# RWKV-7 and windowed-attention block: low-rank decay and rate products over rounded parts, cumulative decay by a VectorE scan

## The chip, the cores and the metric

The kernel runs on one core of a Trainium2 chip. The time is the device time of one execution in microseconds (us), as the median of several executions. A profiled execution is one further execution of which every instruction was recorded. Its engines are PE (matrix products; PEld is its loading of weights), DVE or VectorE, ACT or ScalarE, POOL or GpSimd, and SP, which issues most loads.

## The reference

One decoder block over 512 tokens with 2048 channels: a projection of the normalised input, RWKV-7 time mixing and sliding-window attention in parallel, a gated merge, and a gated convolutional feed-forward layer. The part that matters is the start of the time mixing:

```python
r, k, v, wd, ad, gd = jnp.split(zs, [o1, o2, o3, o4, o5], axis=-1)
w = -jax.nn.softplus(-(w0 + jnp.tanh(wd) @ w2)) - 0.5
decay = jnp.exp(-jnp.exp(w.astype(f32)))
a = jax.nn.sigmoid(a0 + ad @ a2)
g = jax.nn.sigmoid(gd) @ g2
...
state = (state * w_t[:, :, None, :] + sa[..., None] * kb_t[:, :, None, :]
         + v_t[..., None] * k_t[:, :, None, :])
y = jnp.einsum('bhvk,bhk->bhv', state, r_t)
```

`tanh(wd) @ w2` is the low-rank product of the decay (rank 96 to 1024 channels), `ad @ a2` that of the rate (rank 96 to 1024). The kernel works the recurrence in chunks of 64 tokens, for which it needs, in each chunk, the running sum over tokens of the logarithm of the decay, and that sum's exponentials.

## The kernel before

Large products are made from rounded parts. A full-precision matrix is split into a rounded part "hi" (ACT, a copy to the type F32R) and the rest "lo" (DVE, a subtraction), and a product is the sum of three passes: hi with hi, hi with lo, lo with hi. For the projection, SP loads a piece of weights into `raw`, ACT makes `whi` (L254), DVE `wlo` (L255), and PE runs the three passes (L269 to L271) into `acc`. In the text these passes are "the stream". Four buffers each of `raw`, `whi` and `wlo` let loads and splits run ahead.

The kernel first norms and transposes the input, then does attention, then the time mixing, which is the stage of the change, and then the merge, the output product, the up-projection and the down-projection. The time mixing treats the 16 heads in eight pairs, 128 channels each. For a pair there are three steps.

- `early(p)` prepares. It loads `wl`, the pair's slices of the low-rank weights (L556; columns for the decay, the rate and two for the gate), splits the gate's two, projects k, r and v, and forms the decay, the rate and the scaled keys. The decay's product with `thw` (L576) is four full-precision matmuls that put tokens on the partitions; tanh (L578, ACT) and an addition (L579, DVE) follow; four more full-precision matmuls with the constant `tri` (L583) do the running sum inside each chunk and put channels on the partitions; two exponentials (L584 into `Et`, L586 into `Ei`) read it. The rate's product is one full-precision matmul of 512 columns (L589).
- `late(p)` builds the chunk matrices (`BAR`, `BKK`, L625 to L628, multiplied at L645), inverts a triangular matrix by doubling (L697 to L749), and then runs the chain over eight chunks. In each, PE makes `psG` (L757), DVE copies it to `GY` (L758), PE makes `psU` (L760), ACT and DVE copy it to `UV` (L761, L762), PE makes `psS` (L766), and DVE updates the state `SV` (L770). Each step waits for the one before.
- `final(p)` transposes the result (L798), multiplies by the gate (L812) and stores.

`early(p + 1)` is written between `late(p)` and `final(p)`, and a scheduler at build time interleaves the stream, the next pair's preparation and the chain in one fixed order for each engine. Engines run their own instructions in that order, each waiting for what it needs. Six entries of a pair (transposes and first products) are tied by hand to places in the stream (the lists FIRST, LATER and LAST).

`wl` has one buffer. POOL issues loads that add to what is in memory or in SBUF; they prepare sums of weights for later stages (L239) and inside the up-projection (L1102).

Of the kernel before, what the change touches and what calls it, by code (L numbers as in the profile page):

```python
# [18 lines left out]
P = 128  # L19
S = 512  # L20
NT = S // P
HD = 64
C = 64
# [5 lines left out]
SQE = float(np.exp(-0.5))  # L29
# [5 lines left out]
class Dims:  # L35
# [37 lines left out]
CONST_PARTS = (  # L73
    ("ident", 128), ("strict", 64), ("incl", 64), ("istack", 64),
    ("m1", 64), ("m2", 32), ("m4", 32), ("m8", 32), ("m16", 32), ("m32", 32),
    ("t1bd", 128), ("idsg", 128), ("tri", 128), ("bo", 128), ("sel2", 2), ("ones", 128), ("dist", 256),
)
CONST_AT = {}
_at = 0
# [6 lines left out]
def shape_constants():  # L86
    out = np.zeros((P, NCONST), np.float32)

    def put(nm, a):
        o, n = CONST_AT[nm]  # L90
        out[:, o : o + n] = a

    i = np.arange(P)
    put("ident", np.eye(P))
    s = (i % C)[:, None]
    t = np.arange(C)[None, :]
    put("strict", s < t)
    put("incl", s <= t)
    put("istack", SG * (s == t))
    put("idsg", SG * np.eye(P))  # L100
    for m in LEVELS:
        off = (s // (2 * m) == t // (2 * m)) & (s % (2 * m) < m) & (t % (2 * m) >= m)

        put(f"m{m}", SG * off if m == 1 else ((off | (s == t)) / SG)[:, t[0] % (2 * m) >= m])
    si, ti = i[:, None], i[None, :]
    put("t1bd", (si == ti) | ((si // 2 == ti // 2) & (si > ti)))
    same = si // C == ti // C
    put("tri", same & (si <= ti))
    put("bo", same)
    put("sel2", si // C == np.arange(2)[None, :])  # L110
    put("ones", 1.0)
    kj = np.arange(2 * BLK)[None, :]
    dist = (BLK + si - kj).astype(np.float32)
    put("dist", np.where((dist >= 0) & (dist < WIN), -dist, -1e32))
    return out
# [19 lines left out]
def block_kernel(ctx: ExitStack, tc: tile.TileContext, d: Dims, a: dict, out: bass.AP):  # L135
    nc = tc.nc
    act, dve, pool, pe, sync = nc.scalar, nc.vector, nc.gpsimd, nc.tensor, nc.sync
# [40 lines left out]
    K = {nm: cst[:, o - P : o - P + n] for nm, (o, n) in CONST_AT.items() if o}  # L178
# [32 lines left out]
    def split(hi, lo, src, pin=free):  # L211
        pin(act.activation(hi, src, AF.Copy))
        pin(dve.tensor_tensor(lo, src, hi.bitcast(F32) if hi.dtype == F32R else hi, op=ALU.subtract))
# [6 lines left out]
    for f in range(NPRE):  # L220
        w, t = a["w_up"][f], {n: up_d[f, n] for n in ("s3", "s1", "P6", "P3")}
# [70 lines left out]
    if True:  # L292
# [3 lines left out]
        with tc.tile_pool(name="x0_ps", bufs=6, space=PSUM) as ps0:  # L296
            ssum = p0.tile([P, NT], F32, name="ssum")
            HT = NT // 2
            for h in range(2):
# [3 lines left out]
                r = rsqrt_small(p0, ssum[:, h * HT : (h + 1) * HT], 1.0 / d.D, RMS_EPS)  # L303
# [3 lines left out]
            for h in range(2):  # L307
                hs = slice(h * HT * P, (h + 1) * HT * P)
                for k in range(NK):
                    ps = ps0.tile([P, HT * P], F32, name="ps_x", tag="x")  # L310
# [47 lines left out]
        with ExitStack() as pt:  # L358
# [32 lines left out]
            for t in range(NKV):  # L391
# [30 lines left out]
            for g in range(NHK):  # L422
# [7 lines left out]
                for n in range(NT):  # L430
                    ts = slice(n * P, (n + 1) * P)
# [54 lines left out]
        with ExitStack() as pr:  # L486
# [13 lines left out]
            def shifted(acc, mucol, dst, i):  # L500
                z = zpads[i]
                act.activation(z[:, 1:], acc, AF.Identity, scale=pcol[:, mucol : mucol + 1])
                dve.scalar_tensor_tensor(dst, acc, omu[:, mucol : mucol + 1], z[:, 0:S], op0=ALU.mult, op1=ALU.add)

            def wtile(tag, bufs=1):
                return wk.tile([P, S], F32, name=tag, tag=tag, bufs=bufs)

            def bulk():
                return blk.tile([P, S], F32, name="bulk", tag="bulk")

            NG = d.GL // P
            thw = lp.tile([P, S], F32, name="thw")
            adz = lp.tile([P, S], F32, name="adz")
            gdz = [lp.tile([P, NG, S], F32R, name=f"gd{e}") for e in ("hi", "lo")]
            bor = lp.tile([P, P], F32R, name="bor")
            dve.tensor_copy(bor, K["bo"])
            acc = ztile(d.c_wd)
            shifted(acc, PR["muwd"], thw, 0)
            act.activation(thw, thw, AF.Tanh)
            if d.DL < P:  # L520
                dve.memset(thw[d.DL : P], 0.0)
            dve.memset(thw[d.DL : d.DL + 1], 1.0)
            acc = ztile(d.c_ad)
            shifted(acc, PR["muad"], adz, 1)
            if d.AL < P:
                dve.memset(adz[d.AL : P], 0.0)
            for i in range(NG):
                acc = ztile(d.c_gd + i * P)
                t = wtile("lw")
                shifted(acc, PR["mugd"] + i, t, i % 2)  # L530
                act.activation(t, t, AF.Tanh, scale=0.5)
                dve.tensor_scalar(t, t, 0.5, 0.5, op0=ALU.mult, op1=ALU.add)
                split(gdz[0][:, i], gdz[1][:, i], t)
# [17 lines left out]
            def r3(ap, c=C):  # L551
                return ap.rearrange("p (n c) -> p n c", c=c)

            def early(p):
                wl = lp.tile([P, 2 + NG, P], F32, name="wl", tag="wl", bufs=1)
                sync.dma_start(wl, a["lora"][p].rearrange("p (k c) -> p k c", c=P))  # L556
                w2 = wl[:, 0]
                ag = [lp.tile([P, NG, P], F32R, name=f"w{e}", tag=f"w{e}", bufs=2) for e in ("ghi", "glo")]
                split(*ag, wl[:, 2:])

                sums_along(up_jobs)()
                acc = ztile(d.c_k + p * P)
                kz = wtile("kz")
                shifted(acc, PR["mu"] + NP + p, kz, 0)
                kk = wtile("kk")
                dve.tensor_scalar(kk, kz, col("k_k", p), None, op0=ALU.mult)
                sq = wtile("lg")
                act.activation(sq, kk, AF.Square)
                ps = bulk()
                head_stats(ps, sq)  # L570
                rs = rsqrt_small(wk, ps[:, 0 : 2 * NT], None, None, mx=1e-24)
                rb = head_rows(wk, bulk(), rs, "lg")
                ps = bulk()
                for t in range(NT):
                    ts = slice(t * P, (t + 1) * P)
                    pe.matmul(ps[:, ts], thw[:, ts], w2, start=True, stop=True)  # L576
                lg = wtile("lw")
                act.activation(lg, ps, AF.Tanh, scale=0.5)  # L578
                dve.tensor_scalar(lg, lg, 1.0, None, op0=ALU.add)  # L579
                ps = bulk()  # L580
                for t in range(NT):
                    ts = slice(t * P, (t + 1) * P)
                    pe.matmul(ps[:, ts], lg[:, ts], K["tri"], start=True, stop=True)  # L583
                act.activation(Et[:, :, 1:], r3(ps), AF.Exp, scale=-0.5 * SQE)  # L584
                Ei = wtile("Ei")
                act.activation(Ei, ps, AF.Exp, scale=0.5 * SQE)  # L586

                ps = bulk()
                pe.matmul(ps, wl[:, 1], adz, start=True, stop=True)  # L589
                ta = wtile("at_")  # L590
                act.activation(ta, ps, AF.Tanh, scale=0.5, bias=half[:, 0, p : p + 1])

                acc = ztile(d.c_r + p * P)
                rz = wtile("rz")
                shifted(acc, PR["mu"] + p, rz, 1)
                acc = ztile(d.c_v + p * P)
                vz = wtile("vz", 2)
                shifted(acc, PR["mu"] + 2 * NP + p, vz, 0)

                k2 = wtile("k2")  # L600
                dve.tensor_scalar(k2, ta, half[:, 1, p : p + 1], half[:, 2, p : p + 1], op0=ALU.mult, op1=ALU.add)
                dve.tensor_tensor(k2, k2, kz, op=ALU.mult)
                dve.tensor_scalar(ta, ta, 0.5, 0.5, op0=ALU.mult, op1=ALU.add)
                kb = kz
                rk = wtile("lw")
                dve.scalar_tensor_tensor(rk, rz, col("r_k", p), k2, op0=ALU.mult, op1=ALU.mult)
                rkl = [wk.tile([P, S], F32R, name=f"rk{e}", tag="rhl" if e else "dd") for e in range(2)]
                split(*rkl, rk)
                pin(dve.tensor_tensor(kk, kk, rb, op=ALU.mult))
                dve.tensor_tensor(kb, kk, ta, op=ALU.mult)  # L610
                ps = bulk()
                for e in range(2):
                    pe.matmul(ps, bor, rkl[e], start=e == 0, stop=e == 1)
                bon = wtile("bon", 2)
                dve.tensor_tensor(bon, vz, ps, op=ALU.mult)
                return ag, Ei, kk, kb, k2, rz, vz, bon
# [876 lines left out]
```

## Time and profile before

| | us |
|---|---|
| median of 3 runs | 2801.39 |
| lowest and highest | 2800.23, 2801.68 |
| the profiled execution | 2801.0 |
| its span, first to last instruction | 2799.2 |

In the profile, a row of a timeline has the start in us from the span's start, the time that it took, the engine, the line of the kernel, the operation, the tile written and the tiles read, the shape, and how many such instructions follow each other; in brackets stand the idle time of that engine just before, and what ended it. A row of a group has, after the bar, the total busy time in us and the mean of one in ns. Line numbers are those of the kernel before; in the excerpts of the new order they are up to a few lines off for the same statement (L269 to L271 there are L267 to L269, psG, psU and psS are L760, L763 and L769).

### The profile page before, as it was taken

Reading aid. Unit: us, or ns where it says so; the run is one execution under the profiler, and the core shown is the slowest. Engines: PE = TensorE matmul, PEld = TensorE weight load, DVE = VectorE, ACT = ScalarE, POOL = GpSimd, SP = SyncE. Lnnn points to the kernel's source line nnn. Section 1 sums busy time; section 2 is a strip of 40 time slices with the busy share of each in tenths; the row PEclk is TensorE's granted clock in tenths of the full one; section 3 lists DMA queues with packets and bytes.
Section 4 is the critical chain, followed back from the end, with each engine's and each line's share of the span. In section 5 each row is a group of like instructions: output and inputs, shape, how many; then the busy total and the mean of one; then the engine's idle time right before and its main releaser. Section 6 shows DMA issues by size and latency. Waiting matters only on the chain.

```text
span 2799.2 us, 45969 instructions
## 1 busy us (share of the span) xinstructions
PE 2755.7 (98%) x17466; PEld 2401.1 (86%) x17466; DVE 1985.3 (71%) x3452; ACT 1352.1 (48%) x2278; POOL 231.3 (8%) x307
## 2 busy tenths in 40 slices
PE   6999999999999999999999999999999999999999
PEld 5777788888878788888889999999999999888887
DVE  5588677877787774545678778787777778655555
ACT  4355445545544553322466554545555555444444
POOL 0001110110101001011000011101110101000000
PEclk9999999999999999999999999999999999999999
DMA  7865887777777777888776888888888888877775
GB/s 220 229 159 155 210 208 190 194 193 189 197 182 199 186 177 219 239 255 284 248 254 187 234 230 221 241 233 227 229 242 229 225 232 236 317 243 241 256 256 188
DMA packets 227182, 619.62 MB, mean 221 GB/s; under 512 B 24832, under 2 KB 44944, under 8 KB 225936
## 3 DMA queue, kind: packets, MB, share of 16 engines
q1 hardware_dynamic: 158400, 441.03, 48.2%
q0 software_dynamic: 37216, 136.33, 25.5%
q10 hardware_dynamic: 31344, 39.31, 4.0%
q8 instruction: 137, 2.24, 0.3%
q14 instruction: 85, 0.70, 0.1%
HBM read 566.96 MB, written 191.18 MB: 271 GB/s over the span
## 4 chain that ended last, share of the span: by engine, by line
PE 88%; DVE 6%; ACT 2%; issue 1%; DMA 1%; ACTq 0%; SPq 0%; DVEq 0%
PE X L1133 17%; PE X L997 11%; PE acc L271 10%; PE acc L270 10%; PE acc L269 10%; PE Y L997 9%; PE Y L1133 8%; PE Z L1133 4%; PE psS L766 1%; PE psG L757 1%; PE bulk L697 1%; DVE wlo L1116 1%; PE bulk L745 1%; ACT whi L1114 1%; PE psU L760 1%
## 5 line engine op out<-in xcount | busy, mean ns | idle before, releaser
L270 PE MATMUL acc<-xlo,whi 128*128 128x512 f32 x1152 | 461.8, 401 | 0.0
L269 PE MATMUL acc<-xhi,whi 128*128 128x512 f32 x1152 | 459.5, 399 | 1.9 <-DVE xlo L315 1.9
L271 PE MATMUL acc<-xhi,wlo 128*128 128x512 f32 x1152 | 460.7, 400 | 0.3 <-DVE wlo L255 0.3
L254 ACT ACTIVATE whi<-raw 128x512 fp32r<-128x512 f32 x352 | 219.8, 629 | 394.5 <-PE acc L270 298.6
L990 DVE TENSOR_TENSOR wlo<-raw,whi 128x1024 fp32r<-128x1024 f32 x210 | 256.9, 1224 | 199.3 <-ACT whi L989 198.2
L989 ACT ACTIVATE whi<-raw 128x1024 fp32r<-128x1024 f32 x210 | 222.6, 1060 | 282.8 <-PE X L997 147.1
L255 DVE TENSOR_TENSOR wlo<-raw,whi 128x512 fp32r<-128x512 f32 x352 | 240.9, 688 | 151.2 <-ACT whi L254 136.5
L1116 DVE TENSOR_TENSOR wlo<-raw,whi 128x1024 fp32r<-128x1024 f32 x184 | 224.6, 1222 | 77.2 <-ACT whi L1114 77.0
L1133 PE MATMUL X<-b,whi 128*128 128x256 f32 x1472 | 268.9, 283 | 0.2 <-ACT whi L1114 0.2
L1133 PE MATMUL X<-t,whi 128*128 128x256 f32 x1408 | 257.2, 283 | 1.4 <-ACT u L1161 1.4
L1133 PE MATMUL Y<-t,whi 128*128 128x256 f32 x1408 | 257.1, 283 | 0.0
L269 PEld LDWEIGHTS acc<-xhi,whi 128*128 128x128 f32 x1152 | 217.0, 188 | 42.7 <-DVE xlo L315 2.2
L270 PEld LDWEIGHTS acc<-xlo,whi 128*128 128x128 f32 x1152 | 216.9, 188 | 41.8 <-issue 2.0
L271 PEld LDWEIGHTS acc<-xhi,wlo 128*128 128x128 f32 x1152 | 217.0, 188 | 39.4 <-issue 0.9
L1133 PEld LDWEIGHTS X<-b,whi 128*128 128x128 f32 x1472 | 229.6, 192 | 0.4 <-ACT whi L1114 0.4
L1114 ACT ACTIVATE whi<-a 128x1024 fp32r<-128x1024 f32 x124 | 130.9, 1056 | 201.8 <-DVE a L1109 196.4
L1133 PEld LDWEIGHTS X<-t,whi 128*128 128x128 f32 x1408 | 219.6, 192 | 1.6 <-ACT u L1161 1.6
L1133 PEld LDWEIGHTS Y<-t,whi 128*128 128x128 f32 x1408 | 219.6, 192 | 0.0
L1133 PE MATMUL X<-b,wlo 128*128 128x256 f32 x736 | 208.6, 283 | 0.9 <-DVE wlo L1116 0.9
L1114 ACT ACTIVATE whi<-raw 128x1024 fp32r<-128x1024 f32 x184 | 192.9, 1049 | 22.7 <-ACT whi L1114 14.7
L1133 PE MATMUL X<-t,wlo 128*128 128x256 f32 x704 | 199.6, 283 | 0.7 <-DVE wlo L1116 0.7
L1116 DVE TENSOR_TENSOR wlo<-a,whi 128x1024 fp32r<-128x1024 f32 x124 | 151.9, 1225 | 67.5 <-ACT whi L1114 66.9
(387 smaller groups left out, 5795.7 us busy)
## 6 DMA issues: line engine op xcount, KB each, us to landing
raw<-in_w_up_dram SPq DMA_DIRECT2D x170, 512.0 KB
raw<-in_w_z_dram SPq DMA_DIRECT2D x288, 256.0 KB
s_dn<-in_w_dn_dram POOLq DMA_DIRECT2D x88, 512.0 KB, 7.2
raw<-s_dn SPq DMA_DIRECT2D x88, 512.0 KB
raw<-in_w_up_dram POOLq DMA_DIRECT2D x80, 512.0 KB, 8.5
raw<-in_w_dn_dram SPq DMA_DIRECT2D x66, 512.0 KB
s_dn<-in_w_dn_dram SPq DMA_DIRECT2D x44, 512.0 KB
s_dn<-s_dn SPq DMA_DIRECT2D x44, 512.0 KB
```

The costliest lines, as they stand in the source:

```text
L254: act.activation(hi, raw, AF.Copy)
L255: dve.tensor_tensor(lo, raw, hi.bitcast(F32), op=ALU.subtract)
L269: stream.append(pe.matmul(acc, whi[:, j], xhi[:, k], start=first, stop=False))
L270: stream.append(pe.matmul(acc, whi[:, j], xlo[:, k], start=False, stop=False))
L271: stream.append(pe.matmul(acc, wlo[:, j], xhi[:, k], start=False, stop=last))
L697: ins = pe.matmul(ps[:, n], wt[:, 0, n], both(n), start=True, stop=False)
L989: act.activation(whi, wr, AF.Copy)
L990: dve.tensor_tensor(wlo, wr, whi.bitcast(F32), op=ALU.subtract)
L997: pe.matmul(dst, l[:, q, ts], r[:, es], start=fst and j == 0, stop=lst and j == 2, skip_group_check=True)
L1114: pin(act.activation(hi, t, AF.Copy))
L1116: return lambda: pin(dve.tensor_tensor(lo, t, hi.bitcast(F32), op=ALU.subtract))
L1133: pin(pe.matmul(ps, l[:, k], r[:, k], start=start and k + i == 0, stop=last and i == 2, skip_group_check=True))
```

## The change

The decay's and the rate's products become three passes over rounded parts, as in the stream, with channels on the partitions at once. For this `thw` and `adz` are split once at the start into `wad`, and the split of `wl` covers all of its 512 columns. The running sum becomes a scan on DVE over all 512 tokens, in which a row `chunks` of ones, with a zero at each chunk's first token, multiplies the sum so far. The constants `tri` and `ones` go, `thw` and `adz` share buffers with other tiles, and the program is built with `dynamic_dma_scratch_size=8192`, an argument that was not given before.

```diff
-            thw = lp.tile([P, S], F32, name="thw")
-            adz = lp.tile([P, S], F32, name="adz")
+            wad = [lp.tile([P, 2, S], F32R, name=f"wad{e}") for e in ("hi", "lo")]
+            chunks = lp.tile([P, S], F32, name="chunks")
+            dve.memset(chunks, 1.0)
+            dve.memset(chunks.rearrange("p (n c) -> p n c", c=C)[:, :, 0:1], 0.0)
...
+            thw = wtile("lg")
             shifted(acc, PR["muwd"], thw, 0)
             act.activation(thw, thw, AF.Tanh)
...
+            split(*(w[:, 0] for w in wad), thw)
             acc = ztile(d.c_ad)
+            adz = wtile("kz")
             shifted(acc, PR["muad"], adz, 1)
...
+            split(*(w[:, 1] for w in wad), adz)
...
-                w2 = wl[:, 0]
-                ag = [lp.tile([P, NG, P], F32R, name=f"w{e}", tag=f"w{e}", bufs=2) for e in ("ghi", "glo")]
-                split(*ag, wl[:, 2:])
+                parts = [lp.tile([P, 2 + NG, P], F32R, name=f"w{e}", tag=f"w{e}", bufs=2) for e in ("ghi", "glo")]
+                split(*parts, wl)
+                ag = [w[:, 2:] for w in parts]
+
+                def low_rank(i):
+                    ps = bulk()
+                    for j, (l, r) in enumerate(((0, 0), (0, 1), (1, 0))):
+                        pe.matmul(ps, parts[l][:, i], wad[r][:, i], start=j == 0, stop=j == 2)
+                    return ps
...
-                ps = bulk()
-                for t in range(NT):
-                    ts = slice(t * P, (t + 1) * P)
-                    pe.matmul(ps[:, ts], thw[:, ts], w2, start=True, stop=True)
+                ps = low_rank(0)
                 lg = wtile("lw")
                 act.activation(lg, ps, AF.Tanh, scale=0.5)
                 dve.tensor_scalar(lg, lg, 1.0, None, op0=ALU.add)
-                ps = bulk()
-                for t in range(NT):
-                    ts = slice(t * P, (t + 1) * P)
-                    pe.matmul(ps[:, ts], lg[:, ts], K["tri"], start=True, stop=True)
-                act.activation(Et[:, :, 1:], r3(ps), AF.Exp, scale=-0.5 * SQE)
                 Ei = wtile("Ei")
-                act.activation(Ei, ps, AF.Exp, scale=0.5 * SQE)
-
-                ps = bulk()
-                pe.matmul(ps, wl[:, 1], adz, start=True, stop=True)
+                dve.tensor_tensor_scan(Ei, chunks, lg, 0.0, op0=ALU.mult, op1=ALU.add)
+                act.activation(Et[:, :, 1:], r3(Ei), AF.Exp, scale=-0.5 * SQE)
+                act.activation(Ei, Ei, AF.Exp, scale=0.5 * SQE)
+
+                ps = low_rank(1)
...
-    nc = _bacc.Bacc("TRN2", target_bir_lowering=False, num_devices=1)
+    nc = _bacc.Bacc("TRN2", target_bir_lowering=False, num_devices=1, dynamic_dma_scratch_size=8192)
```

The built order moves at three places of which the prediction speaks. The first is PE in the chain of a settled pair, at the second and third chunk, where the next pair's low-rank products stand. Before:

```order
L576 MATMUL bulk<-wl,thw 128x128 x3
L766 MATMUL psS<-UV,W_2937 128x64 x2
L576 MATMUL bulk<-wl,thw 128x128
L270 MATMUL acc<-xlo,whi 128x512
L271 MATMUL acc<-xhi,wlo 128x512
L269 MATMUL acc<-xhi,whi 128x512
L757 MATMUL psG<-SV,BAR 128x64 x2
L270 MATMUL acc<-xlo,whi 128x512
L583 MATMUL bulk<-cst,lw 128x128 x2
L760 MATMUL psU<-GY,BX 128x128
L583 MATMUL bulk<-cst,lw 128x128 x2
L589 MATMUL bulk<-adz,wl 128x512
```

The same place after the change, from the last pass of the decay's product on:

```order
L568 MATMUL bulk<-wadhi,wglo 128x512
L769 MATMUL psS<-UV,W_2946 128x64 x2
L568 MATMUL bulk<-wadhi,wghi 128x512
L568 MATMUL bulk<-wadlo,wghi 128x512
L568 MATMUL bulk<-wadhi,wglo 128x512
L268 MATMUL acc<-xlo,whi 128x512
L760 MATMUL psG<-SV,BAR 128x64 x2
L269 MATMUL acc<-xhi,wlo 128x512
L267 MATMUL acc<-xhi,whi 128x512
L268 MATMUL acc<-xlo,whi 128x512
L269 MATMUL acc<-xhi,wlo 128x512
L763 MATMUL psU<-GY,BX 128x128
```

The rate's passes moved up between psS and psG, and four passes of the stream stand between psG and psU where one pass and two L583 products stood.

The second place is DVE at the same chunks. Before:

```order
L762 COPY UV<-psU 64x64
L770 SCALAR_TENSOR_TENSOR SV<-SV,ee,psS 64x64 x2
L579 TENSOR_SCALAR lw<-lw 128x512
L758 COPY GY<-psG 128x128
L762 COPY UV<-psU 64x64
L770 SCALAR_TENSOR_TENSOR SV<-SV,ee,psS 64x64 x2
```

After (the scan is printed as SCALAR_TENSOR_TENSOR with `Ei` as its output):

```order
L765 COPY UV<-psU 64x64
L773 SCALAR_TENSOR_TENSOR SV<-SV,ee,psS 64x64 x2
L586 TENSOR_SCALAR lw<-lw 128x512
L588 SCALAR_TENSOR_TENSOR Ei<-chunks,lw 128x512
L761 COPY GY<-psG 128x128
L604 TENSOR_SCALAR k_7345<-at__7187,half 128x512
L605 TENSOR_TENSOR k_7345<-k_7345,kz 128x512
L765 COPY UV<-psU 64x64
```

The scan stands between the addition and the copy to `GY`, and two operations on `k` moved ahead of the copy to `UV`.

The third place is SP's queue of loads at the start of the stage, where it issues `wl` of the second pair. Before:

```order
L238 DMA s_o_99<-s_o_91 128x1024
L251 DMA raw<-in_w_z_dram 128x512
L350 DMA rsd<-rsT 8x128
L354 DMA rsb<-rsd 64x512 x2
L556 DMA wl<-in_lora_dram 128x512
L238 DMA s_u_147<-in_w_up_dram 128x1024
```

After:

```order
L236 DMA s_o_93<-s_o_89 128x1024
L560 DMA wl<-in_lora_dram 128x512
L249 DMA raw<-in_w_z_dram 128x512
L236 DMA s_u_147<-in_w_up_dram 128x1024
L249 DMA raw<-in_w_z_dram 128x512
L560 DMA wl<-in_lora_dram 128x512
```

The second pair's `wl` moved from behind the first pair's row sums (`rsd`, `rsb`) to a place thirteen rows ahead of them, and the third pair's follows it closely.

More of the change, by code (lines that the diff above doesn't have):

```diff
@@ L75 @@
     ("m1", 64), ("m2", 32), ("m4", 32), ("m8", 32), ("m16", 32), ("m32", 32),
-    ("t1bd", 128), ("idsg", 128), ("tri", 128), ("bo", 128), ("sel2", 2), ("ones", 128), ("dist", 256),
+    ("t1bd", 128), ("idsg", 128), ("bo", 128), ("sel2", 2), ("dist", 256),
 )
@@ L107, in shape_constants @@
     same = si // C == ti // C
-    put("tri", same & (si <= ti))
     put("bo", same)
     put("sel2", si // C == np.arange(2)[None, :])
-    put("ones", 1.0)
     kj = np.arange(2 * BLK)[None, :]
```

## The prediction

> **What bounds the kernel now.** I read the page's parts 1 and 4 first, for the engine that sets the end.
>
> ```profile
> span 2799.2 us, 45969 instructions
> PE 2755.7 (98%) x17466; PEld 2401.1 (86%) x17466; DVE 1985.3 (71%) x3452; ACT 1352.1 (48%) x2278; POOL 231.3 (8%) x307
> PE 88%; DVE 6%; ACT 2%; issue 1%; DMA 1%; ACTq 0%; SPq 0%; DVEq 0%
> ```
>
> PE is busy for 98% of the span and holds 88% of the chain of waits. That is an average, so I cut the span at the stage that the change touches, with the view that sums stretches. Each row has a stretch, its length, then busy time (and count) of PE, PEld, DVE, ACT and POOL, the granted clock, DMA share and GB/s.
>
> ```profile
> 280.00:330.00 50.00, 49.42 (x226) 39.87 (x225) 25.90 (x53) 19.70 (x35) 6.69 (x8) 1.00 0.89 237
> 330.00:423.60 93.60, 91.24 (x612) 73.35 (x613) 76.12 (x184) 44.51 (x100) 9.09 (x12) 1.00 0.79 195
> 520.50:616.80 96.30, 95.88 (x638) 77.47 (x637) 74.69 (x183) 48.06 (x106) 9.46 (x14) 1.00 0.75 192
> ```
>
> 280 to 330 holds the first pair's preparation, 520.5 to 616.8 one settled pair. In the settled pair PE idles 96.30 - 95.88 = 0.42 us, at full clock, while VectorE works 78% of the time. So a microsecond of PE work taken out here is a microsecond off the end, unless PE then arrives early at something that is not ready. Only the first pair has PE idle to win, 2.4 us.
>
> **PE work, per pair.** The timeline of PE around the removed products shows start, length, and what ran. A matmul's length overlaps the next one, so its cost is the distance between starts.
>
> ```profile
> 389.31 0.39 PE L270 MATMUL acc<-xlo,whi 128*128 128x512 f32 x1
> 389.54 0.39 PE L271 MATMUL acc<-xhi,wlo 128*128 128x512 f32 x1
> 389.77 0.40 PE L269 MATMUL acc<-xhi,whi 128*128 128x512 f32 x1
> 390.00 0.39 PE L270 MATMUL acc<-xlo,whi 128*128 128x512 f32 x1
> 390.23 0.55 PE L757 MATMUL psG<-SV,BAR 128*128 128x64 f32 x4
> ...
> 391.58 0.61 PE L583 MATMUL bulk<-cst,lw 128*128 128x128 f32 x4
> 392.02 1.02 PE L589 MATMUL bulk<-adz,wl 128*128 128x512 f32 x2
> 392.88 0.55 PE L766 MATMUL psS<-UV,W 128*128 128x64 f32 x4
> ```
>
> A product of rounded parts with 512 columns takes (390.23 - 389.31) / 4 = 0.23 us. Four records of L583 take 392.02 - 391.58 = 0.44 us, 0.11 each, and I cost those of L576, of the same shape and median length, alike. The two of L589 take 392.88 - 392.02 = 0.86 us. How many there are, over eight pairs (the three numbers are shortest, median and longest ns):
>
> ```profile
> L576 PE MATMUL bulk<-wl,thw x64: 273/275/328, 310.2 to 968.0; 128*128 128x128 f32 x64
> L583 PE MATMUL bulk<-cst,lw x64: 271/275/348, 312.5 to 970.5; 128*128 128x128 f32 x64
> L589 PE MATMUL bulk<-adz,wl x16: 592/594/595, 313.5 to 971.1; 128*128 128x512 f32 x16
> ```
>
> The code has four, four and one per pair; the trace has two records for each, since a full-precision product runs twice. Out per pair: 8 x 0.11 (L576) + 8 x 0.11 (L583) + 0.86 (L589) = 2.62 us. In: two groups of three products of rounded parts, 6 x 0.23 = 1.38 us. Net 1.24 us a pair, 9.9 us over eight.
>
> **What the scan does to the chain.** The matmul with "tri" is replaced by a scan on VectorE, in order with everything else there. Behind it in VectorE's queue stands the copy GY (the second order excerpt), and the next psU on PE waits for GY. No scan is in the trace. The nearest rows are two-input operations of full precision:
>
> ```profile
> L990 DVE TENSOR_TENSOR wlo<-raw,whi 128x1024 fp32r<-128x1024 f32 x210 | 256.9, 1224 | 199.3 <-ACT whi L989 198.2
> L255 DVE TENSOR_TENSOR wlo<-raw,whi 128x512 fp32r<-128x512 f32 x352 | 240.9, 688 | 151.2 <-ACT whi L254 136.5
> ```
>
> One such operation over 512 columns takes 0.69 us, which is the floor; two one after the other, for the multiply and the add, take 1.38, the ceiling. I take 1.22, the 1024-column row, because each column's add must be done before the next column's multiply can start, so I count two steps a column in one instruction. [...]
>
> Now the place. These are rows of the chain of an earlier settled pair on PE, ACT and DVE:
>
> ```profile
> 581.46 0.83 PE L576 MATMUL bulk<-wl,thw 128*128 128x128 f32 x6
> 582.25 0.66 PE L766 MATMUL psS<-UV,W 128*128 128x64 f32 x4
> 582.75 0.44 PE L576 MATMUL bulk<-wl,thw 128*128 128x128 f32 x2
> ...
> 584.89 0.39 PE L760 MATMUL psU<-GY,BX 128*128 128x128 f32 x2
> 583.23 0.60 ACT L578 ACTIVATE lw<-bulk 128x512 f32<-128x512 f32 x1 [1.46 <-PE bulk L576]
> 582.95 0.59 DVE L770 SCALAR_TENSOR_TENSOR SV<-SV,ee,psS 64x64 f32<-64x64 f32 x2 [0.75 <-PE psS L766]
> 583.86 0.43 DVE L579 TENSOR_SCALAR lw<-lw 128x512 f32<-128x512 f32 x1 [0.32 <-ACT lw L578]
> 584.36 0.29 DVE L758 COPY GY<-psG 128x128 f32<-128x128 f32 x1
> ```
>
> The tanh L578 starts 0.04 us after the last L576 ends. In the new order the first group starts at 581.46, its third product ends at 581.46 + 2 x 0.23 + 0.39 = 582.31, so tanh runs to 582.95. VectorE does SV until 583.54 as now, L579 until 584.0, a scan of 1.22 until 585.2, GY until 585.5. PE does psS from 582.25 (0.45), the second group (0.69), one stream product (0.23), psG (0.45), then four stream products (0.92), allowing 0.08 for each return from full precision to the stream: psU could start at 585.1. It waits 0.45 us. With a scan of 0.69 GY ends at 585.0 and nothing waits; with 1.38 the wait is 0.6. Seven pairs have this chain beside the preparation: 7 x 0.45 = 3.2 us given back (0 to 4.2). Behind GY the next items on VectorE are k's two operations and the second copy of UV; five stream products (1.15 us) stand between psU and the psS that needs it, which about covers them.
>
> **The first pair.** Here PE does wait today. The queue that loads weights (SP) issues the second "wl" late, since its buffer is held by the full-precision products and it stands behind the row-sum loads.
>
> ```profile
> 317.76 0.55 SPq L556 DMA_DIRECT2D wl<-in_lora_dram  x1
> 323.47 0.42 ACT L212 ACTIVATE wghi<-wl 128x256 fp32r<-128x256 f32 x1 [4.30 <-DMA wl<-in_lora_dram]
> 323.92 0.43 DVE L213 TENSOR_TENSOR wglo<-wl,wghi 128x256 fp32r<-128x256 f32 x1 [3.66 <-ACT wghi L212]
> 331.48 1.97 PE L645 MATMUL bulk<-BAR,BKK 128*128 128x256 f32 x8 [1.99 <-DVE BAR L627]
> 334.90 1.99 PE L645 MATMUL bulk<-BAR,BKK 128*128 128x256 f32 x8 [0.54 <-DVE bon L615]
> ```
>
> ACT stands 4.30 us for that load, VectorE 3.66 us for ACT, and PE 1.99 + 0.54 us for VectorE. After the change "wl" is free as soon as it is split, and its second load and split stand ahead of the preparation (the third excerpt). VectorE then reaches BAR about 3.7 us sooner, PE only 1.24 us sooner: I take both waits away, 2.5 us (0 if the load's wait returns). What is late next is ACT at the new place of that split. There it is covered:
>
> ```profile
> 281.93 0.42 ACT L212 ACTIVATE wghi<-wl 128x256 fp32r<-128x256 f32 x1 [3.03 <-DMA wl<-in_lora_dram]
> 291.87 0.63 ACT L254 ACTIVATE whi<-raw 128x512 fp32r<-128x512 f32 x1 [2.09 <-PE acc L270]
> ```
>
> The same wait of 3.03 us passed at 282 with no PE idle, and ACT has 2.09 us spare before a "whi", waiting for PE to free its buffer. Without that cover each microsecond of the load's delay would be PE's. SP's weight loads queue behind the moved "wl" too; they run ahead by the same spare buffers.
>
> **The rest** I put at nothing. The wider split costs VectorE 0.69 instead of 0.43 and ACT 0.63 instead of 0.42; with the scan VectorE has 74.7 + 1.5 of some 95 us. Without that slack it would cost the 1.5 us a pair. The two new splits and two memsets at the start, about 4 us of VectorE, meet 25.9 busy of 50. The exponentials read SBUF instead of PSUM at like length. Dropping "tri" and "ones" shortens a load at the very start.
>
> **Sum.** 9.9 + 2.5 - 3.2 = 9.2 us. The profiled run took 2801.0 around its span of 2799.2; 2801.0 - 9.2 = 2791.8. The median 2801.4 is 0.4 over that run, so 2792.2.
>
> **Rivals.**
>
> The scan is cheap or hidden: 9.9 + 2.5, so 2789.0. For it: VectorE idles 0.75 and 0.32 us in the rows above. Against: the feedback from column to column. Chance 0.17.
>
> The chain takes the gain back: its eight steps, not PE, become the limit where preparation and chain overlap. The settled pair's 0.42 us of idle says that PE and chain are closely matched, and with 1.24 us less to fill, PE would only wait longer. Then seven pairs gain nothing and the first gains 1.24 + 2.5: 2797.7. Against: in the built order 37 stream products still stand behind the last psS of a settled pair (44 before), so the filler was moved and not used up. Chance 0.20.
>
> Slower: the program's DMA scratch size is set to 8192. If loads issued from POOL then have to wait for room, the place is the up-projection, whose accumulating loads go that way.
>
> ```profile
> POOL raw L1102 <- DMA raw<-in_w_up_dram: 391.8, 43, 16.6
> raw<-in_w_up_dram POOLq DMA_DIRECT2D x80, 512.0 KB, 8.5
> ```
>
> At 0.25 us of PE delay for each of 80 loads the price is 20 us: 2801.4 - 9.2 + 20 = 2812. It decides from 15 / 80 = 0.19 us each. Against it: POOL waited 43 times, up to 16.6 us, for an earlier load to land, so few are in flight. [...] Chance 0.10.
>
> **How the numbers follow.** The forecast has 0.53. Its own bounds, scan 0.69 to 1.38 and the first pair's wait gone or kept, run from 2801.4 - 12.4 = 2789.0 to 2801.4 - (9.9 - 4.2) = 2795.7. The range 2786 to 2800 adds the case of the chain and 3 us below for waits that the new order may happen to remove, and leaves out the slower case. About 0.2% (5.6 us) is what a measurement of this kernel can tell from no change. Faster than 2795.8: 0.53 x 0.95 + 0.17 + 0.20 x 0.15 = 0.70; within: 0.20; slower: 0.10.
>
> **What would show it.** Right: six records a pair of 0.23 us where 18 were; a scan near 1.2 us; psU waiting some 0.4 us on GY once a pair; settled pairs of about 95.5 us; no wait of PE at the first L645. Wrong: a pair still at 96.3 us with PE idle behind VectorE; a scan over 2 us; new PE waits on DMA after 1500 us; or the wait for "wl" reappearing as PE idle near 290 us.

## The result, and the profile after

| | us |
|---|---|
| before, median of 6 runs beside the change | 2801.34 (2799.43 to 2804.69) |
| after, median of 6 runs | 2819.91 (2810.47 to 2825.40) |
| ratio, 95% interval | 1.0063 (1.0053 to 1.0073) |
| profiled execution after, its span | 2817.49, 2815.7 |

The change makes the kernel 0.6% slower, 18.6 us by the medians, where 9.2 us less was forecast. The page's first and fourth parts, after:

```profile
span 2815.7 us, 45783 instructions
PE 2757.2 (98%) x17370; PEld 2397.6 (85%) x17370; DVE 1999.6 (71%) x3464; ACT 1354.6 (48%) x2280; POOL 231.8 (8%) x307
PE 83%; DVE 8%; DMA 4%; ACT 3%; issue 1%; SPq 0%; ACTq 0%; DVEq 0%
```

PE has 96 instructions fewer, as it should (12 a pair), and is still 98% busy. The busy share hides the loss; the chain of waits shows more of it: PE went from 88% to 83% of it, and DMA from 1% to 4%.

To see where the 16.5 us between the spans came in, I cut both spans at the same events: the first stream product at the stage's start, the copy to `rsT` for the second pair, and the first stream product after the stage. Before, then after (stretch, length, busy PE, PEld, DVE, ACT, POOL, clock, DMA share, GB/s):

```profile
280.96:387.33 106.37, 103.69 (x643) 83.36 (x642) 72.47 (x162) 52.97 (x109) 11.52 (x14) 1.00 0.84 212
387.33:1301.05 913.72, 911.05 (x5529) 738.87 (x5528) 635.12 (x1473) 404.40 (x862) 94.04 (x128) 1.00 0.77 204
1301.05:2799.19 1498.14, 1487.87 (x10073) 1382.91 (x10071) 1087.02 (x1279) 764.69 (x994) 100.94 (x126) 1.00 0.80 238
```
```profile
280.40:391.38 110.98, 103.79 (x630) 84.27 (x628) 75.10 (x166) 54.43 (x111) 12.18 (x15) 0.97 0.83 214
391.38:1316.53 925.15, 910.00 (x5445) 732.51 (x5444) 645.86 (x1480) 404.06 (x860) 93.60 (x127) 1.00 0.75 200
1316.53:2815.73 1499.20, 1488.66 (x10073) 1382.89 (x10071) 1087.26 (x1279) 765.69 (x994) 101.25 (x126) 1.00 0.81 238
```

The first pair lost 4.6 us where 3.7 were to be won (2.5 + 1.24), and the other pairs lost 11.4 us where 5.5 were to be won (7 x 1.24 - 3.2). The 1500 us behind the stage changed by 1.1 us. Two of PE's waits in the stage are new and large, those at L339 and for `UV`; behind the second stands a new wait of VectorE (waiter, waited for, us in total, times, longest):

```profile
PE bulk L339 <- ACT lg L578: 7.1, 1, 7.1
PE psS L769 <- DVE UV L765: 6.9, 4, 3.0
PE psU L763 <- DVE GY L761: 2.2, 7, 0.3
DVE kk L612 <- DMA rsb<-rsd: 8.2, 5, 3.2
```

**The clock.** With its 96 instructions fewer PE is busy 1.5 us longer than before (2755.7). In three stretches of the stage the granted clock is 0.50:

```profile
310.47:317.30 6.83, 4.70 (x15) 4.12 (x16) 3.87 (x17) 1.23 (x3) 0.82 (x1) 0.50 0.92 203
600.60:604.01 3.41, 3.41 (x13) 2.98 (x12) 2.17 (x5) 0.25 (x1) 0.00 (x0) 0.50 0.03 8
798.58:801.99 3.41, 3.41 (x12) 2.83 (x12) 2.17 (x6) 0.22 (x1) 0.00 (x0) 0.50 0.23 44
```

The first stretch begins inside PE's wait of 7.10 us, which ends at 312.60. The others come 1.4 and 1.8 us behind waits of 2.08 and 2.97 us. In the first, five stream products from 314.90 on start 0.43 us apart instead of 0.23. Half of the 11.52 us that PE is busy at this clock, 5.8 us, is an estimate of the price. The kernel with both moves undone (below) has as many PE instructions in the stage and no such stretch there, and its PE is busy 5.88 us less (1.64 in the first pair, 4.24 in the others). So about a third of the loss is slower work behind the waits. In the kernel before, a wait of 2.39 us that ends at 181.38 has no such stretch behind it; what decides it, the runs do not show.

**The first pair.** The timeline of ACT, then of SP, around 290 us:

```profile
294.32 0.63 ACT L210 ACTIVATE wghi<-wl 128x512 fp32r<-128x512 f32 x1 [6.26 <-DMA wl<-in_lora_dram]
...
304.43 0.63 ACT L252 ACTIVATE whi<-raw 128x512 fp32r<-128x512 f32 x1 [4.57 <-DMA raw<-in_w_z_dram]
309.34 0.63 ACT L252 ACTIVATE whi<-raw 128x512 fp32r<-128x512 f32 x1 [4.28 <-DMA raw<-in_w_z_dram]
309.88 0.67 ACT L500 ACTIVATE zpad<-acc,par 128x512 f32<-128x512 f32 x1
```
```profile
286.37 0.53 SPq L560 DMA_DIRECT2D wl<-in_lora_dram  x1
...
288.90 0.36 SPq L249 DMA_DIRECT2D raw<-in_w_z_dram  x1
295.71 0.33 SPq L560 DMA_DIRECT2D wl<-in_lora_dram  x1
296.31 0.33 SPq L249 DMA_DIRECT2D raw<-in_w_z_dram  x1
```

ACT comes to the second pair's `wl` at 288.1 and stands 6.26 us, since that load, issued at 286.37, is there only at 294.3. In the trace this load stands sixteen loads ahead of the first pair's `rsd`. Nothing needs the split before the second pair's low-rank products, the first of which starts at 391.00, beside that pair's `rsT` copy. Behind this split in ACT's order stand those of the stream. SP meanwhile stands at the third `wl`, whose buffer comes free with that split, and issues it at 295.71; the stream's next weights go out behind it, from 296.31 on. The loads run dry: ACT waits 4.57 and 4.28 us for `raw`, the shift L500 behind it comes at 309.88, and PE stands 7.1 us at the row sums (L339).

**The later pairs.** The chain of waits through the fourth `rsT` copy (start, us, what), and VectorE's rows at its end:

```profile
585.99 0.28 DVE rsT L346
...
586.29 4.17 DMA rsd<-rsT
...
591.04 6.50 DMA rsb<-rsd
...
597.64 0.69 DVE kk L612
```
```profile
594.44 0.29 DVE L761 COPY GY<-psG 128x128 f32<-128x128 f32 x1
...
597.64 0.69 DVE L612 TENSOR_TENSOR kk<-kk,rsb 128x512 f32<-128x512 f32 x1 [2.30 <-DMA rsb<-rsd]
...
598.96 0.23 DVE L765 COPY UV<-psU 64x64 f32<-64x64 f32 x1
```

The row sums go out to memory and come back spread over the partitions; `kk` needs them. From the copy to the start of `kk` it takes 11.65 us here. VectorE stands 2.30 us for it, and the copy to `UV`, a step of the chain, is queued behind. The same place before:

```profile
581.66 0.28 DVE L348 COPY rsT<-bulk 8x128 f32<-8x128 f32 x1 [0.73 <-PE bulk L346]
...
592.52 0.29 DVE L758 COPY GY<-psG 128x128 f32<-128x128 f32 x1
...
593.32 0.68 DVE L609 TENSOR_TENSOR kk<-kk,rsb 128x512 f32<-128x512 f32 x1
594.04 0.23 DVE L762 COPY UV<-psU 64x64 f32<-64x64 f32 x1
```

There `kk` came 11.66 us behind the `rsT` copy, without a wait. That the two figures agree is chance: before, the last semaphore update of the second read came at 592.72, 11.06 us behind the copy. The way is not of one length. From the copy to that update it took 7.5 to 11.2 us in the last six pairs before, and 8.5 to 12.5 in the change. Before, `kk` stood 11.65 or 11.66 us behind the copy in each of these six; the read was there 0.5 and 0.6 us earlier in two of them and 3.5 to 4.1 us earlier in four. In the change `kk` comes 9.24 us behind the copy where it does not wait (686.04 to 695.28), and it waits in the five others.

The copy to `GY` ahead of `kk` was that of the fifth chunk before; in the new order it is that of the fourth. One chunk step less lies between the transfer's start and the instruction that needs its end.

### The profile page after: what moved, and what is told of

Same layout as the page of the kernel before. It is cut to its first block, busy times and chain, and to the rows that moved or that the text cites. A ratio compares the mean times of both kernels' runs of the same rounds, so it can differ in the third digit from the quotient of the medians.

```text
span 2815.7 us, 45783 instructions
## 1 busy us (share of the span) xinstructions
PE 2757.2 (98%) x17370; PEld 2397.6 (85%) x17370; DVE 1999.6 (71%) x3464; ACT 1354.6 (48%) x2280; POOL 231.8 (8%) x307
## 4 chain that ended last, share of the span: by engine, by line
PE 83%; DVE 8%; DMA 4%; ACT 3%; issue 1%; SPq 0%; ACTq 0%; DVEq 0%
PE X L1136 17%; PE X L1000 10%; PE acc L269 9%; PE acc L267 9%; PE acc L268 9%; PE Y L1000 9%; PE Y L1136 8%; PE Z L1136 4%; DVE wlo L253 1%; DMA rsb<-rsd 1%; PE psS L769 1%; PE bulk L648 1%; DMA raw<-in_w_z_dram 1%; PE bulk L700 1%; PE psG L760 1%
```

## The experiments

Each kernel ran beside the one before on the same chip, in five rounds; ratios are to it, with 95% intervals.

**Undoing the two moves.** An order was tied by hand at one or both places; arithmetic and instructions stay as in the change. `behind(a, b)` orders `a` after `b` on its own engine without a wait; `rowsum` and `gy` hold the row-sum reads and the copies to `GY` as they were issued.

```diff
# wl behind the row-sum reads of the pair before
+                if rowsum:
+                    behind(load, rowsum[-1])
# kk behind the copy to GY of the fifth chunk
+                ins = pin(dve.tensor_tensor(kk, kk, rb, op=ALU.mult))
+                if gy:
+                    behind(ins, gy[4])
```

> The changed kernel, with each pair's load of wl put back behind the previous pair's row-sum loads in SP's queue, as in the kernel before; nothing else moves. The theory that the first pair lost its time to the early split of the second wl (ACT stood 6.3 us for that load, and SP stood until 295.7 us for the buffer): the 7.1 us wait of PE before the first pair's row sums goes, and the time falls by 5 to 7 us from the changed kernel's 2819.9, to about 2813 to 2815. The rival that the first pair is late for another reason, or that the wait only comes back later at the first chunk matrices (as in the kernel before, 2.5 us): 0 to 3 us less, 2817 to 2820.

> The changed kernel, with VectorE's product of kk with rsb put behind the copy to GY of the fifth chunk, where it stood before, instead of the fourth. The theory that DVE now waits for the row-sum round trip with the chain behind it (8.2 us over five pairs, 6.9 us of them seen by PE at psS): the wait for rsb goes and the time falls by 6 to 8 us, to about 2812 to 2814, with less spread between runs. The rival that the settled pairs are slow because of the scan and not of rsb: the wait for rsb goes but the time stays within 2 us, 2818 to 2821.

> Both edits together: wl behind the row-sum loads, kk behind the fifth chunk's GY. If the two losses are separate and add: 2819.9 - 13 = 2806 to 2808, still slower than the 2801.3 before, because a settled pair without a wait for rsb had 1.6 us more of small PE stalls, more than the 1.24 us taken from PE. If those small stalls too came from the two moves, 2795 or less.

| | median us | ratio |
|---|---|---|
| the change | 2819.91 | 1.0063 (1.0053 to 1.0073) |
| wl back | 2807.62 | 1.0024 (1.0015 to 1.0033) |
| kk back | 2808.53 | 1.0024 (1.0014 to 1.0034) |
| both back | 2800.39 | 0.9999 (0.9990 to 1.0008) |

Each tie gave back 11 to 12 us, more than expected, and both together 19.5, less than their sum; of the two outcomes expected for both, 2806 to 2808 and 2795 or less, neither came. A part of the reason is in the waits. With `wl` back VectorE's waits for `rsb` shrank too, and with `kk` back PE's wait in the first pair did:

```profile
DVE kk L616 <- DMA rsb<-rsd: 5.9, 3, 2.6
```
```profile
PE bulk L339 <- ACT lg L579: 5.0, 1, 5.0
```

The first row is of `wl` back (8.2 in the change), the second of `kk` back (7.1). The clock is another part, which the expectations did not count: `kk` back keeps a stretch at 0.50 in the first pair (310.70 to 317.52), `wl` back has one at 789.39 to 792.80, and with both back the stage has none. Each run has one profile, so I don't split the rest of the difference. With both back both waits are gone, and the whole loss with them: two places in the order cost the 0.6%. The stretches of that kernel, cut as above:

```profile
282.02:385.51 103.49, 102.15 (x630) 82.27 (x628) 75.27 (x165) 54.54 (x111) 11.35 (x14) 1.00 0.85 219
385.51:1298.41 912.90, 905.76 (x5445) 729.76 (x5444) 645.15 (x1480) 404.19 (x860) 94.59 (x128) 1.00 0.76 204
```

The first pair is now 2.9 us shorter than before (106.37). That is near the 3.7 forecast by luck: the forecast rests on an early second `wl`, which this kernel puts back late, and PE still waits 1.1 us for `bon` at the first chunk matrices. In the seven kernels of this section that put `wl` back in the change, PE's waits there come to 1.1 to 3.2 us, and the first pair takes 103.5 to 106.7. The seven others, 912.90 us against 913.72, have won only 0.8 of the 8.7 us of PE work taken out.

**Load or split?** The early second `wl` does two things: SP carries it early, and ACT stands for it. With `kk` back, ACT's half of each split was ordered behind the square (`sqs`) for the row sums of the pair before; the second load kept its early place in SP's queue.

```diff
-                split(*parts, wl)
+                ins = act.activation(parts[0], wl, AF.Copy)
+                dve.tensor_tensor(parts[1], wl, parts[0].bitcast(F32), op=ALU.subtract)
+                if sqs:
+                    behind(ins, sqs[-1])
```

> The changed kernel with kk behind the fifth GY (2808.5), and with ACT's half of the split of each wl put behind the square for the row sums of the pair before; the second wl's load keeps its new early place in SP's queue. If the first pair's loss is that ACT, in order, stands 6.3 us for a load that has no need to be there yet, it goes without touching the load: 2800 to 2803. If the loss is that SP's queue carries this load ahead of the stream's weights, the stream still starves: 2806 or more.

Measured: 2800.23 us, 0.9996 (0.9987 to 1.0005), 8 us less than with `kk` back alone. The first pair:

```profile
282.67:384.62 101.95, 101.84 (x630) 82.36 (x628) 75.08 (x165) 54.95 (x111) 12.03 (x15) 1.00 0.88 232
```

At 101.95 us with 0.1 of PE idle it is the shortest of all runs: the early load does no harm, and without a wait at the first chunk matrices it wins more than the 3.7 us forecast. What cost the time was that engines stood in order for a load long before its result was needed. The third `wl` moved later with the split (from 295.81 with `kk` back alone to 310.55), so SP's stand for the buffer went in the same edit; the run doesn't part it from ACT's. The whole kernel is no faster than with both moves undone.

**What the scan costs.** With both moves undone, the scan was replaced by one product of the same operands, on the same order of all engines; this leaves out the running sum.

```diff
-                dve.tensor_tensor_scan(Ei, chunks, lg, 0.0, op0=ALU.mult, op1=ALU.add)
+                dve.tensor_tensor(Ei, chunks, lg, op=ALU.mult)
```

> Both edits, and the scan (1.23 us) replaced by one product of the same operands (about 0.69 us); all engines' orders are the same as in the kernel with both edits. It leaves out the running sum of the decay. If the scan's length is on the chain through GY, as the prediction has it (0.45 us a pair, seven pairs), the time falls by about 3 us from the kernel with both edits. If the scan stands beside other work, it stays within 1 us.

Measured: 2796.20 us, 0.9982 (0.9973 to 0.9991), 4.2 us less by the medians. A settled pair, from the `rsT` copy of the fourth pair to that of the fifth, before, then with the scan, then with the short operation:

```profile
581.66:677.90 96.24, 95.86 (x637) 77.41 (x636) 74.62 (x183) 48.05 (x107) 9.78 (x13) 1.00 0.75 192
```
```profile
579.25:675.43 96.18, 95.22 (x624) 76.04 (x623) 76.21 (x184) 48.16 (x107) 9.90 (x13) 1.00 0.76 192
```
```profile
577.21:672.86 95.65, 95.00 (x624) 76.04 (x623) 75.73 (x183) 48.12 (x107) 9.74 (x13) 1.00 0.75 193
```

So 0.53 us less on VectorE (1.22 to 0.69) are 0.53 us of the pair. With the scan, PE in this pair shows where:

```profile
582.49 0.39 PE L269 MATMUL acc<-xhi,wlo 128*128 128x512 f32 x1
583.21 0.49 PE L771 MATMUL psU<-GY,BX 128*128 128x128 f32 x2 [0.33 <-DVE GY L769]
```

From start to start `psU` comes 0.72 us behind the product ahead of it; with the short operation each `psU` comes 0.23 behind. So 0.49 of the 0.53 us is PE's wait for the `GY` behind the scan. The bracket shows only 0.33, since a stream product counts as busy for 0.39 us while the next can start after 0.23.

The next four kernels tried to win that with the scan kept: the scan behind the third chunk's `GY`; that, with the transposes at the end of a pair tied three stream products later; and, with the scan at its place, one or two small VectorE operations done by ACT.

```diff
# scan behind GY
+                if gy:
+                    behind(ins, gy[2])
# and the last tied entry later
-            LATER = (24, ZT + 2, ZT + 31, 2 * ZT + 10, 2 * ZT + 35, 3 * ZT + 14, 5 * ZT + 43)
+            LATER = (24, ZT + 2, ZT + 31, 2 * ZT + 10, 2 * ZT + 35, 3 * ZT + 14, 5 * ZT + 46)
# the addition by ACT
-                dve.tensor_scalar(lg, lg, 1.0, None, op0=ALU.add)
+                act.activation(lg, lg, AF.Copy, bias=1.0)
# and the rate's scaling
-                dve.tensor_scalar(ta, ta, 0.5, 0.5, op0=ALU.mult, op1=ALU.add)
+                act.activation(ta, ta, AF.Copy, scale=0.5, bias=0.5)
```

> The kernel with both moves undone (2800.4), and the scan put behind the copy to GY of the third chunk on VectorE instead of ahead of it, its length unchanged. If the scan's price (0.52 us a settled pair by the run with the short operation) is that GY and then psU wait for it, it goes: settled pairs near 95.6 us instead of 96.16, 2796 to 2797. The rival that 1.23 us more of VectorE work costs wherever it stands, since each chain step has VectorE work queued: within 1 us of 2800.4.

> The same, and in addition the last of the entries tied by hand (the transposes at the end of a pair, which wait 0.3 us a pair for VectorE's yc) is tied three stream products later. If that wait is only a matter of the tied place, 0.3 us a pair go, 2 us over seven pairs, to about 2794 to 2795. The rival: what follows the transposes (the gate's product, the store) then comes later and the wait moves, no change from the run beside it.

> Both moves undone (2800.4), and the addition of 1 to the tanh, 0.43 us on VectorE ahead of the scan, done by ACT. If any microsecond of VectorE work beside the chain is a microsecond of a settled pair (the short operation: 0.54 us less work, 0.52 us a pair), pairs go from 96.16 to near 95.75, and the time to 2797 to 2798. If only the scan's own place counts, no change, and with ACT's longer way to the scan rather more: 2800 to 2802.

> The same, and the scaling of the rate to 0.5 x + 0.5 (0.42 us on VectorE) done by ACT too. By the theory of VectorE work another 0.4 us a pair: pairs near 95.35, 2794 to 2795. By the rival no change from the run beside it.

| | median us | ratio |
|---|---|---|
| scan behind GY | 2803.51 | 1.0005 (0.9997 to 1.0014) |
| and the entry later | 2802.88 | 1.0007 (0.9998 to 1.0016) |
| addition by ACT | 2801.15 | 1.0000 (0.9991 to 1.0009) |
| and the scaling | 2801.97 | 0.9999 (0.9990 to 1.0007) |

None of the four won the 0.5 us a pair. For the last three the rival outcome came, no gain; the first fell outside both of its outcomes. With the scan behind `GY`, PE's waits for `GY` (2.2 us over the seven pairs with the scan ahead) went, and a wait for the next step stood in their place:

```profile
PE psS L779 <- DVE UV L775: 1.6, 7, 0.3
```

With the addition on ACT the waits for `GY` went to 0.2 us too, and VectorE had 0.4 us less to do, but the pair stayed at 96.26:

```profile
581.06:677.32 96.26, 95.51 (x624) 76.08 (x623) 75.84 (x183) 48.62 (x108) 9.83 (x13) 1.00 0.75 192
```

My theory that any VectorE microsecond beside the chain is a microsecond of the pair falls with that. What is won at `psU` comes back at later steps, by the same distances between starts. With the scan behind `GY`, three `psS` come 0.61, 0.41 and 0.40 us behind the stream product ahead instead of 0.23 to 0.27. With the addition on ACT, `psU` comes 0.36 behind instead of 0.72, but one `psS` 0.41 and a product of `BAR` and `BKK` 0.48 instead of 0.23. Why nothing comes back with the short operation, the runs leave open.

**One product alone.** First the kernel before with only the rate's product as passes and the scratch size of 8192, then the change with the rate's product back in full precision. In both, the product that stays reads `wl` until late.

```diff
# rate alone, on the kernel before
+                for j, (l, r) in enumerate(((0, 0), (0, 1), (1, 0))):
+                    pe.matmul(ps, parts[l][:, 0], wad[r], start=j == 0, stop=j == 2)
-                pe.matmul(ps, wl[:, 1], adz, start=True, stop=True)
# decay alone, on the change
-                ps = low_rank(1)
+                ps = bulk()
+                pe.matmul(ps, wl[:, 1], adz, start=True, stop=True)
```

> The kernel before, with the rate's product alone as three passes (0.86 us out, 0.69 in) and the DMA scratch size of 8192; decay and running sum as before. The second wl's load stays behind the first pair's row-sum write, but stands ahead of the row-sum reads; kk stays behind the fifth GY. PE work falls by 1.4 us over eight pairs. If the scratch size or the passes themselves cost nothing: 2799 to 2801. If the load ahead of the row-sum reads makes kk wait as in the changed kernel: 2803 or more, with a wait of kk for rsb in the trace.

> The changed kernel, with the rate's product in full precision again (0.69 us a pair of passes out, 0.86 in). wl is held by that product until late, so that its next load goes back behind the row-sum write by itself, though ahead of the row-sum reads; kk stays at its early place behind the fourth GY. The theory of two moves: the first pair's 7 us wait goes, the waits of kk for rsb stay: 2808 to 2815. The rival that the loss comes from the decay's passes and the scan as such: no less than 2818.

The rate alone: 2799.03 us, 0.9992 (0.9983 to 1.0001), the time of the first outcome, but with `kk` waiting 2.1 us for `rsb` as in the second. The decay alone: 2811.55, 1.0038 (1.0022 to 1.0053), with 3.5 us of such waits and no wait at the first row sums. VectorE's waits in the rate alone and in the decay alone:

```profile
DVE kk L613 <- DMA rsb<-rsd: 2.1, 4, 0.7
```
```profile
DVE kk L612 <- DMA rsb<-rsd: 3.5, 3, 1.8
```

In the order of the first, `kk` kept its place, in that of the second it is at the early one, while the second `wl` is late in both. So it is the decay's part that draws `kk` forward by a chunk, and the two together that free `wl` early. Last, the rate alone with `wl` behind the row-sum reads:

```diff
+                if rowsum:
+                    behind(load, rowsum[-1])
```

> The kernel before with the rate's product alone as passes (2799.0, with 2.1 us of waits of kk for rsb over four pairs), and the load of wl behind the row-sum reads, as in the kernel before. If the load ahead of those reads is what makes kk wait there, the waits go and three or four pairs gain 0.5 us: 2797 to 2798, less what the first pair gives back where that load comes later (2.9 us faster than before in the run without this tie). If the waits are chance of the loads in flight, no change: 2799.

Measured: 2801.48 us, 0.9997 (0.9988 to 1.0006). The waits of `kk` for `rsb` went, as expected of a load moved from ahead of those reads, and a settled pair is 0.4 us shorter than before (95.83 against 96.24). The time did not follow, and came above both of its outcomes: neither of these two is clear of the kernel before. No run that computes the whole block beats it.

## Why the prediction was wrong

**PE work: right within 0.15 us a pair.** Two of the rate's passes and the stream product behind them stand in the trace 0.23 us apart, as costed:

```profile
587.36 0.39 PE L568 MATMUL bulk<-wadlo,wghi 128*128 128x512 f32 x1
587.59 0.40 PE L568 MATMUL bulk<-wadhi,wglo 128*128 128x512 f32 x1
587.82 0.40 PE L268 MATMUL acc<-xlo,whi 128*128 128x512 f32 x1
```

The first pass of that group started 0.32 us before the first of these rows. It follows a full-precision product, `psS`; over the stage, the first stream product behind a `psS` also stands 0.32 us ahead of the next by the median, and one behind another stream product 0.23. In the settled pair with both moves undone the six passes take 1.65 us from start to start (1.38 forecast), and the products that they replace took 2.74 before (2.62): net 1.09 instead of 1.24.

**The scan: right in length, a little low in price.** Forecast 1.22 us:

```profile
L588 DVE TENSOR_TENSOR_SCAN Ei<-chunks,lw 128x512 f32<-128x512 f32 x8 | 9.8, 1224 | 0.3
```

That is 1.8 times the two-input operation of the same width (0.69), so the row of 1024 columns was the right neighbour. That each column takes two steps was my estimate; the trace shows the length alone. The forecast price was a wait of 0.45 us of `psU` for `GY` (its own rounded times, 585.5 and 585.1, give 0.4); the trace shows 0.49, and the short operation 0.53 of the pair.

**The first pair: wrong, and this step failed: "What is late next is ACT at the new place of that split. There it is covered".** I took the cover from a wait of 3.03 us on another `wl` and from 2.09 us that ACT had spare before one `whi`. The wait was 6.26. The prediction also said that without cover each microsecond would be PE's; that came true, and at more than its length: against the kernel with the split alone held back, the first pair has 7.1 us more of PE idle and 1.95 more of PE busy (103.79 against 101.84), the latter at the lower clock. What I left out is SP: the third `wl` follows the second closely in the order I showed, and must stand for the same split. That the gain itself was there the run with the split alone held back shows: its first pair is 4.4 us shorter than before, and PE has no wait at the first chunk matrices.

**"The rest I put at nothing": wrong.** The orders moved more than the three places that I costed. `kk` went ahead of the fourth chunk's `UV`, and I did not ask what it waits for. In the trace before, it showed no wait, and I took that for slack. It stood 11.66 us behind the `rsT` copy where the way through memory took up to 11.2; the change brought it to 9.24, where that way took up to 12.5. That way is of two transfers one after the other, and with less PE work beside it it was no shorter here, while everything I took out of PE or let move up brings `kk` closer to the copy. The sum also had no term for a lower clock behind a wait (0.50 for 3.4 to 6.8 us in three stretches). Of the small items in that paragraph, the two splits and two memsets at the start took 1.9 us of VectorE instead of about 4, and the exponentials took 0.63 and 0.62 us from SBUF against 0.60 and 0.59 from PSUM before.

**The rivals.** That the chain takes the gain back (0.20, 2797.7) is what the kernel with both moves undone does: settled pairs of 96.18 us against 96.24, a gain in the first alone, 2800.39. It had a better claim than my forecast, beneath the two losses. My own condition, "unless PE then arrives early at something that is not ready", is what came. `psU`'s wait of 0.49 us explains less than half of the 1.18 that a settled pair does not win. The rest is small waits; over the stage, PE's for `XIW` and `yc` were, before and with both moves undone:

```profile
PE bulk L697 <- DVE XIW L213: 1.4, 6, 0.2
...
PE bulk L798 <- DVE yc L791: 0.3, 1, 0.3
```
```profile
PE bulk L707 <- DVE XIW L211: 2.4, 7, 0.4
...
PE bulk L809 <- DVE yc L802: 2.0, 7, 0.6
```

These grew by 2.7 us together. From start to start, in the settled pair, the transposes of `yc` come 0.61 us behind the product ahead instead of 0.23, and the `XIW` product that waits longest 0.75 instead of 0.64. With `psU`'s wait that is 0.98 of the 1.18 us; what sets the last 0.2 stays open. The slower rival, loads of POOL that wait for room with the scratch size at 8192, did not come: the stretch after the stage grew by 1.1 us, not 20, and the kernel with the rate alone, built with 8192, is not slower than before. That such loads wait for room at this size at all was a supposition of mine, which no run shows. I gave slower 0.10 and had the sign wrong by a mechanism that was on none of my lists, although one of its two halves stood under "Wrong": the wait for `wl` reappearing near 290 us.

## What to carry to other kernels

When an edit lets an instruction move up in an in-order queue, price what it waits for at the new place, and who stands behind it. Here 1.09 us of PE work came out of a settled pair, while the row sums' way through memory took 8.5 to 12.5 us in the last six pairs, after 7.5 to 11.2 before. An instruction that waits for nothing in the profile may have little slack (0.5 us in two of six pairs here): measure from the landing of what it needs to its own start, in every pair. Where PE stands, look at the granted clock behind the wait too (0.50 in three stretches here, 11.52 us of busy PE). On a kernel where PE is 98% busy, a chain that runs beside it can still set the pair's length, so that work taken from PE turns into small waits (96.18 us against 96.24 with both moves undone).

## What the runs showed of the hardware

In the fourth pair of the change a write of 4 KB to memory took 4.17 us to land and the second of the reads that wait for it (each to 64 partitions of 512 numbers) 6.50, beside loads of weights, with the core's DMA engines moving 195 GB/s (585.99 to 597.64 us). Over the eight pairs before, from issue to the last semaphore update, the write took 1.7 to 5.4 us and a read 2.8 to 6.3. All of these are issued by SP.

From 289.26 to 295.71 us SP stood 6.45 us for the buffer of the third `wl`, and the next load of the stream's weights went out behind that, at 296.31.

The change also spreads its runs: 2810.47 to 2825.40, 15 us, where the kernel with both moves undone has 6.4 (2797.36 to 2803.76). The mean granted clock of a run goes with it: 0.998 in the run of 2810.47 us and 0.994 to 0.996 in the three above 2822; with both moves undone it is 0.997 to 1.000. That waits on transfers, with the lower clock behind them, make this spread fits, but no run tested it.
